# Turning probabilities and values in pieces between the weight splits of a two-layer decoder

## The chip, the cores and the metric

The kernel runs on one core of one Trainium2 chip, as one program that is launched once. The metric is the device time of that launch in microseconds (us). Five engines work side by side, each through its own list of instructions in the order in which they stand: TensorE (PE in the profile; PEld are its loads of stationary operands), VectorE (DVE), ScalarE (ACT), GpSimd (POOL) and SyncE (SP), which issues most of the transfers from memory. An engine that waits for a semaphore holds up everything that stands behind in its list.

## The reference

A decoder trunk of two layers over 272 tokens (16 learned ones and 256 of the sequence), width 2048, 16 heads of 128, feed-forward width 8192, all float32. The first layer mixes tokens by softmax attention with a decay that is learned per token, the second by stick-breaking attention; both compute blocks of queries against all keys up to the block's end. Cut to what matters here:

```python
for layer in range(DEPTH):                       # 2
    a = rms_norm(h, norm_attn[layer])
    if layer < N_A_LAYERS:                       # layer 0
        q, k, v, f_logit = split(a @ fox_w_in)
        cum_logf = cumsum(log_sigmoid(f_logit + fox_b_f))
        o = forgetting_attention(q, k, v, cum_logf)    # softmax(q k * scale + decay) @ v
        h = h + o @ fox_w_o
    else:                                        # layer 1
        c = rms_norm(h, kv_norm)
        k, v = split(c @ w_kv)
        q = a @ sb_w_q
        o = stick_breaking_attention(q, k, v)    # exp(log_sigmoid(z) + suffix sums) @ v
        h = h + o @ sb_w_o
    h = h + square(relu(rms_norm(h, norm_mlp[layer]) @ w_up[layer])) @ w_down[layer]
return rms_norm(h, final_norm)[:, N_META:]
```

## The kernel before

Activations lie feature-major: 16 chunks of 128 features by 272 tokens. All products with weights go through `gemm_group`, which makes 4 output chunks (512 columns of weights, `acc`) from all 16 input chunks, in four quarters `kb` of four input chunks each. A float32 product is made of three products of rounded parts: each weight tile `raw` is split by ACT into a rounded part `whi` (L214) and by DVE into the rest `wlo` (L215), the activations likewise into `hi` and `lo`, and PE adds hi*hi, lo*hi and hi*lo (L162). So a quarter is 4 x 4 x 3 = 48 matmuls. A quarter's weights come as two halves of 512 KB, by SP, into 4 `raw` buffers; there are 4 `whi` and 4 `wlo` buffers, so that ACT and DVE split at most two quarters ahead of PE. Quarters 0 and 3 finish one output chunk after the other, so they need both halves early; quarters 1 and 2 use one half and then the other.

Heads go in four groups `g` of four. In layer 0 a group has three gemm groups, for queries, keys and values; in layer 1 two, for keys and values, since all queries are made ahead. After the keys come the scores of the group's heads and, beside the values' gemm, the softmax or the stick-breaking sums on DVE and ACT. Both the probabilities and the values then stand the wrong way round for the product that makes the heads' outputs and are turned:

- `turned`: DVE turns each 32 x 32 square within its partitions (`sb`, L346, two instructions), then ACT moves the 16 squares of a 128 x 128 block to their places with 16 copies (`pt`, L350), each 32 partitions x 384.
- `token_major`: when the values' gemm is read out of PSUM (`vT`, L357), DVE turns them with 16 transposes of 32 x 256 (`vt`, L365).

`outputs` then multiplies `vt` by `pt` on PE (`po`, L384 to L388) and splits the result into the next operand (`x_o`, L408 and L409). It is not run at once: `small` (the corners, that is the 16 learned tokens and the last keys) and `outputs` are kept in `late`. In layer 0 `small` is queued ahead of quarter 2 of the next group of queries, and `outputs` behind that group; in layer 1, and in both out-projections, they go ahead of quarters 1 and 3 of the next gemm group.

What sets the order: each engine's list is made by a scheduler that runs when the program is built. It takes ready instructions by the order of the code and by a modelled time; `issue_after` adds that an instruction must stand behind a given one on the same engine. `gemm_group` takes functions `before` and `after` by quarter; those in `after` are traced once a quarter's splits are, under `issue_after` of that quarter's last `whi` and last `wlo`:

```python
if kb in after:
    with tc.issue_after(on_act.ins), tc.issue_after(on_dve.ins):
        after[kb]()
```

Before the change all 32 instructions of a turning are traced at one place, the copies ahead of the values' gemm and the transposes behind it.

## Time and profile before

| | us |
|---|---|
| median of 3 runs | 2320.24 |
| lowest and highest run | 2319.99, 2321.96 |
| the profiled execution | 2322.33 |
| its span, first to last instruction | 2320.6 |
| PE busy | 2280.8 |
| DVE busy | 1359.6 |
| ACT busy | 1110.3 |

The profile is of one execution. The time that the kernel is judged by is some 1.7 us longer than the span, since it holds what lies ahead of the first and behind the last instruction. A row of the timeline gives start, length, engine, line and what is written from what, and in brackets the idle time of the engine just before and what ended it. Of PE's matmuls a row's length overlaps the next one's; the pace is read from start to start. A few matmul records are missing from a trace. The granted clock of PE is given as a share of its full clock.

### The profile page before, as it was taken

What the parts mean: (1) busy time and instruction counts of PE and PEld (TensorE: products, weight loads), DVE (VectorE), ACT (ScalarE), POOL (GpSimd) and SP (SyncE); (2) the same over time, 40 slices, a digit from 0 to 9 for tenths busy, and PEclk for the clock granted to TensorE, in tenths of its full rate; (3) what the DMA queues carried; (4) which work ended last, traced back from release to release, by engine and by line L of the source; (5) the groups of instructions that cost most, each with busy time, mean ns of one, the idle gap of its engine ahead of it and who ended that gap; (6) DMA issues with size and microseconds to landing.
All of it is one profiled execution on the core that took longest, in us unless ns stands there. A gap on an engine that the chain in (4) does not pass through costs nothing.

```text
span 2320.6 us, 44744 instructions
## 1 busy us (share of the span) xinstructions
PE 2280.8 (98%) x18882; PEld 2272.9 (98%) x18882; DVE 1359.6 (59%) x1909; ACT 1110.3 (48%) x1533; POOL 27.5 (1%) x75
## 2 busy tenths in 40 slices
PE   9899999999999999999999999999999999999998
PEld 9899999999999999999999999999999999999998
DVE  7766666654455445455566677776555555555554
ACT  6553554444344345334444566655543544544553
POOL 1000000000000000000000000000000000000000
PEclk9999999999999999999999999999999999999999
DMA  7445444555555555555555544456566566565563
GB/s 239 147 147 174 155 145 160 184 168 187 176 176 182 171 186 175 183 171 184 173 182 189 177 153 146 147 172 198 184 200 193 189 200 192 191 200 191 191 200 128
DMA packets 116905, 412.32 MB, mean 178 GB/s; under 512 B 13520, under 2 KB 16992, under 8 KB 116704
## 3 DMA queue, kind: packets, MB, share of 16 engines
q1 hardware_dynamic: 114560, 406.29, 54.2%
q8 instruction: 148, 2.42, 0.4%
q10 hardware_dynamic: 2144, 3.17, 0.4%
q14 instruction: 53, 0.43, 0.1%
HBM read 407.29 MB, written 2.11 MB: 176 GB/s over the span
## 4 chain that ended last, share of the span: by engine, by line
PE 92%; DVE 2%; ACT 1%; issue 1%; DVEq 0%; ACTq 0%
PE acc L162 90%; DVE vt L365 1%; ACT pt L350 1%; DVE wlo L215 1%; PE po L384 1%; PE ps L338 0%; PE po L387 0%; PE ps L336 0%; DVE sb L346 0%; ACT whi L214 0%; PE po L388 0%; DVE ob L668 0%; DVE vT L357 0%; PE pms_fin L625 0%; DVE ob L665 0%
## 5 line engine op out<-in xcount | busy, mean ns | idle before, releaser
L215 DVE TENSOR_TENSOR wlo<-raw,whi 128x1024 fp32r<-128x1024 f32 (+1 forms) x773 | 926.6, 1216 | 714.3 <-ACT whi L214 707.4
L214 ACT ACTIVATE whi<-raw 128x1024 fp32r<-128x1024 f32 (+1 forms) x773 | 795.9, 1050 | 986.0 <-PE acc L162 935.2
L162 PE MATMUL acc<-x_m,whi 128*128 128x272 f32 (+1 forms) x4096 | 643.3, 282 | 0.0
L162 PE MATMUL acc<-x_u,whi 128*128 128x272 f32 (+1 forms) x4096 | 642.9, 282 | 0.0
L162 PEld LDWEIGHTS acc<-x_m,whi 128*128 128x128 f32 x4096 | 566.1, 188 | 0.1
L162 PEld LDWEIGHTS acc<-x_u,whi 128*128 128x128 f32 x4096 | 565.9, 188 | 0.0
L162 PE MATMUL acc<-x_m,wlo 128*128 128x272 f32 (+1 forms) x2048 | 441.1, 282 | 0.0
L162 PE MATMUL acc<-x_u,wlo 128*128 128x272 f32 (+1 forms) x2048 | 441.0, 282 | 0.0
L162 PE MATMUL acc<-x_a,whi 128*128 128x272 f32 (+1 forms) x2048 | 362.1, 290 | 8.8 <-ACT whi L214 8.8
L162 PEld LDWEIGHTS acc<-x_m,wlo 128*128 128x128 f32 x2048 | 323.5, 188 | 0.0
L162 PEld LDWEIGHTS acc<-x_u,wlo 128*128 128x128 f32 x2048 | 323.4, 188 | 0.0
L162 PEld LDWEIGHTS acc<-x_a,whi 128*128 128x128 f32 x2048 | 307.9, 193 | 10.1 <-ACT whi L214 9.9
L162 PE MATMUL acc<-x_a,wlo 128*128 128x272 f32 (+1 forms) x1024 | 258.0, 290 | 9.4 <-DVE wlo L215 9.4
L162 PE MATMUL acc<-x_kv,whi 128*128 128x272 f32 x1024 | 195.5, 290 | 0.0
L162 PEld LDWEIGHTS acc<-x_a,wlo 128*128 128x128 f32 x1024 | 179.8, 192 | 11.2 <-DVE wlo L215 10.8
L162 PE MATMUL acc<-x_o,whi 128*128 128x272 f32 (+1 forms) x1024 | 162.6, 283 | 0.7 <-ACT x_o L408 0.4
L162 PEld LDWEIGHTS acc<-x_kv,whi 128*128 128x128 f32 x1024 | 162.6, 191 | 0.0
L162 PE MATMUL acc<-x_kv,wlo 128*128 128x272 f32 x512 | 149.0, 291 | 8.1 <-DVE wlo L215 8.1
L162 PEld LDWEIGHTS acc<-x_o,whi 128*128 128x128 f32 x1024 | 141.9, 188 | 1.4 <-DVE x_o L409 0.7
L244 DVE TENSOR_TENSOR hT<-acc,hT 128x272 f32<-128x272 f32 (+1 forms) x160 | 69.0, 431 | 85.6 <-PE acc L162 85.4
L162 PE MATMUL acc<-x_o,wlo 128*128 128x272 f32 (+1 forms) x512 | 110.8, 282 | 2.1 <-DVE wlo L215 2.1
L162 PEld LDWEIGHTS acc<-x_kv,wlo 128*128 128x128 f32 x512 | 98.0, 191 | 8.7 <-DVE wlo L215 8.7
(180 smaller groups left out, 1057.9 us busy)
## 6 DMA issues: line engine op xcount, KB each, us to landing
raw<-w_up SPq DMA_DIRECT2D x256, 512.0 KB, 4.6
raw<-w_dn SPq DMA_DIRECT2D x256, 512.0 KB, 4.6
raw<-w_qkv SPq DMA_DIRECT2D x92, 512.0 KB, 4.1
raw<-w_o SPq DMA_DIRECT2D x64, 512.0 KB, 4.6
raw<-w_kv SPq DMA_DIRECT2D x64, 512.0 KB, 4.5
raw<-w_q SPq DMA_DIRECT2D x32, 512.0 KB, 4.8
fk<-f_dram ACTq DMA_DIRECT2D x4, 544.0 KB, 4.4
raw<-w_qkv SPq DMA_DIRECT2D x7, 256.0 KB, 4.5
```

The costliest lines, as they stand in the source:

```text
L162: ins = nc.tensor.matmul(*args, **kw).ins
L214: on_act = nc.scalar.activation(hp, src, AF.Copy)
L215: on_dve = nc.vector.tensor_tensor(out=lp, in0=src, in1=hp.bitcast(F32), op=ALU.subtract)
L244: nc.vector.tensor_tensor(out=hT[:, c, t0:], in0=acc, in1=hT[:, c, t0:], op=ALU.add)
L350: nc.scalar.activation(out[32 * b:32 * b + 32, :, 32 * a:32 * a + 32], sb[32 * a:32 * a + 32, :, 32 * b:32 * b + 32], AF.Copy)
L365: nc.vector.transpose(out=out[32 * b:32 * b + 32, :, :, 32 * a:32 * a + 32], in_=src[32 * a:32 * a + 32, :, :, 32 * b:32 * b + 32])
L384: ins = nc.tensor.matmul(po[:, i, :], v[:, j, 0, :], p[:, j, :2 * P], start=i == 0, stop=False)
```

## The change

`turned` and `token_major` no longer issue their instructions; each returns the output tile and a function `piece(first, last)` that issues the copies or transposes first to last. A table `PLANS` says which piece goes behind the splits of which quarter. In layer 0 copies 0 to 3 and 4 to 7 go behind quarters 2 and 3 of the group's own values gemm, the other eight behind quarters 0 and 1 of the following gemm group; in layer 1 copies 0 to 3 behind quarter 3 and the rest behind quarters 0 to 2 of the following group. The transposes go behind quarters 0, 1 and 2 of the following group: 4, 6 and 6 in layer 0, and 2, 7 and 7 in layer 1. The two DVE instructions that make `sb` go with the first copies. What follows the last group of heads is the out-projection's first gemm group. `small` and `outputs` keep their places.

```diff
+        def piece(first, last):
+            if first == 0:
+                for o, u, n in ((0, 0, P), (144, P, 2 * P)):
+                    nc.vector.transpose(out=sb.rearrange("p (h k) -> p h k", h=4)[:, :, u:u + n], in_=s[:, :, o:o + n])
+            for i in range(first, last):
+                a, b = 32 * (i // 4), 32 * (i % 4)
+                nc.scalar.activation(out[b:b + 32, :, a:a + 32], src[a:a + 32, :, b:b + 32], AF.Copy)
+
+        return pt.rearrange("p (h k) -> p h k", h=4), piece
...
-        for a in range(4):
-            for b in range(4):
-                nc.vector.transpose(out=out[32 * b:32 * b + 32, :, :, 32 * a:32 * a + 32],
-                                    in_=src[32 * a:32 * a + 32, :, :, 32 * b:32 * b + 32])
-        return vt.rearrange("p h (b t) -> p h b t", t=P)
+
+        def piece(first, last):
+            for i in range(first, last):
+                a, b = 32 * (i // 4), 32 * (i % 4)
+                nc.vector.transpose(out=out[b:b + 32, :, :, a:a + 32], in_=src[a:a + 32, :, :, b:b + 32])
+
+        return vt.rearrange("p h (b t) -> p h b t", t=P), piece
+
+    def early(turn_p, plan):
+
+        return {kb: (lambda a=a, b=b: turn_p(a, b)) for kb, (a, b) in plan.items()}
+
+    def turns(turn_p, turn_v, p, v):
+
+        def piece(kb):
+            if kb in p:
+                turn_p(*p[kb])
+            if kb in v:
+                turn_v(*v[kb])
+
+        return {kb: (lambda kb=kb: piece(kb)) for kb in range(3)}
+
+    PLANS = {0: ({2: (0, 4), 3: (4, 8)}, {0: (8, 12), 1: (12, 16)}, {0: (0, 4), 1: (4, 10), 2: (10, 16)}),
+             1: ({3: (0, 4)}, {0: (4, 8), 1: (8, 12), 2: (12, 16)}, {0: (0, 2), 1: (2, 9), 2: (9, 16)})}
...
-            gemm_group(w_qkv0[3 * g], xa, 0, evac_q, {2: late[0]})
+            gemm_group(w_qkv0[3 * g], xa, 0, evac_q, {2: late[0]}, turning)
...
-        gemm_group(w_qkv0[3 * g + 2], xa, 0, evac_v)
+        gemm_group(w_qkv0[3 * g + 2], xa, 0, evac_v, after=early(turn_p, PLANS[0][0]))
...
+        turning = turns(turn_p, turn_v, *PLANS[0][1:])
...
-            gemm_group(w[g], ao, t0, evac, {1: late[0], 3: late[1]} if g == 0 else {}, widen=t0 == M)
+            gemm_group(w[g], ao, t0, evac, {1: late[0], 3: late[1]} if g == 0 else {},
+                       turning if g == 0 else {}, widen=t0 == M)
```

The calls in layer 1 change in the same way, with `PLANS[1]`.

The built lists show where the pieces come to stand. In their names the numbers of a split are gemm group, quarter and half, and a buffer's number; `pt_0_1` is layer 0, g=1. First ACT in layer 0 at g=1, from the last quarter of the values' gemm (group 6) into the next group of queries (7). Before:

```order
L214 ACTIVATE whi_6_3_0_2037<-raw_6_3_0_2033 128x1024
L350 ACTIVATE pt_0_1_1829<-sb_0_1_1828 32x12x32 x16
L214 ACTIVATE whi_6_3_1_2041<-raw_6_3_1_2034 128x1024
L214 ACTIVATE whi_7_0_0_2129<-raw_7_0_0_2125 128x1024
L214 ACTIVATE whi_7_0_1_2133<-raw_7_0_1_2126 128x1024
L214 ACTIVATE whi_7_1_0_2189<-raw_7_1_0_2185 128x1024
L214 ACTIVATE whi_7_1_1_2193<-raw_7_1_1_2186 128x1024
```

And now:

```order
L214 ACTIVATE whi_6_3_0_2025<-raw_6_3_0_2021 128x1024
L353 ACTIVATE pt_0_1_1829<-sb_0_1_1828 32x12x32 x4
L214 ACTIVATE whi_6_3_1_2029<-raw_6_3_1_2022 128x1024
L353 ACTIVATE pt_0_1_1829<-sb_0_1_1828 32x12x32 x4
L214 ACTIVATE whi_7_0_0_2105<-raw_7_0_0_2101 128x1024
L214 ACTIVATE whi_7_0_1_2109<-raw_7_0_1_2102 128x1024
L353 ACTIVATE pt_0_1_1829<-sb_0_1_1828 32x12x32 x4
L214 ACTIVATE whi_7_1_0_2173<-raw_7_1_0_2169 128x1024
L214 ACTIVATE whi_7_1_1_2177<-raw_7_1_1_2170 128x1024
L353 ACTIVATE pt_0_1_1829<-sb_0_1_1828 32x12x32 x4
```

The sixteen copies stood ahead of the split of the second half of quarter 3; now four stand ahead of it, and the others behind three later splits or pairs of splits.

DVE at the same place, from the read-out of the values (`vT`) to the splits of the next group's quarter 3. Before:

```order
L357 TENSOR_TENSOR vT0_1_1848<-acc_6_3_1852,rstd_a0_542 128x272
L215 TENSOR_TENSOR wlo_7_1_0_2190<-raw_7_1_0_2185,whi_7_1_0_2189 128x2x512
L365 STREAM_TRANSPOSE vt_0_1_2102<-vT0_1_1848 32x4x2x32 x16
L215 TENSOR_TENSOR wlo_7_1_1_2194<-raw_7_1_1_2186,whi_7_1_1_2193 128x2x512
L215 TENSOR_TENSOR wlo_7_2_0_2264<-raw_7_2_0_2259,whi_7_2_0_2263 128x2x512
L215 TENSOR_TENSOR wlo_7_2_1_2268<-raw_7_2_1_2260,whi_7_2_1_2267 128x2x512
L215 TENSOR_TENSOR wlo_7_3_0_2324<-raw_7_3_0_2319,whi_7_3_0_2323 128x2x512
```

And now:

```order
L360 TENSOR_TENSOR vT0_1_1830<-acc_6_3_1834,rstd_a0_542 128x272
L215 TENSOR_TENSOR wlo_7_1_0_2174<-raw_7_1_0_2169,whi_7_1_0_2173 128x2x512
L370 STREAM_TRANSPOSE vt_0_1_2094<-vT0_1_1830 32x4x2x32 x4
L215 TENSOR_TENSOR wlo_7_1_1_2178<-raw_7_1_1_2170,whi_7_1_1_2177 128x2x512
L370 STREAM_TRANSPOSE vt_0_1_2094<-vT0_1_1830 32x4x2x32 x6
L215 TENSOR_TENSOR wlo_7_2_0_2258<-raw_7_2_0_2253,whi_7_2_0_2257 128x2x512
L215 TENSOR_TENSOR wlo_7_2_1_2262<-raw_7_2_1_2254,whi_7_2_1_2261 128x2x512
L370 STREAM_TRANSPOSE vt_0_1_2094<-vT0_1_1830 32x4x2x32 x6
L215 TENSOR_TENSOR wlo_7_3_0_2324<-raw_7_3_0_2319,whi_7_3_0_2323 128x2x512
```

The sixteen transposes stood between the two halves of quarter 1; now four stand there, six behind the pair and six behind quarter 2.

DVE in layer 1 at g=1, from the read-out of the values into the next group of keys (57). Before:

```order
L357 TENSOR_TENSOR vT1_1_15403<-acc_56_3_15407,rstd_a1_13533 128x272
L365 STREAM_TRANSPOSE vt_1_1_15655<-vT1_1_15403 32x4x2x32 x16
L215 TENSOR_TENSOR wlo_57_1_0_15752<-raw_57_1_0_15747,whi_57_1_0_15751 128x2x512
L215 TENSOR_TENSOR wlo_57_1_1_15756<-raw_57_1_1_15748,whi_57_1_1_15755 128x2x512
L374 TENSOR_TENSOR pm_sb_1_1_15742<-pm_1_1_15740,maskD_127 128x128
L215 TENSOR_TENSOR wlo_57_2_0_15812<-raw_57_2_0_15807,whi_57_2_0_15811 128x2x512
L215 TENSOR_TENSOR wlo_57_2_1_15816<-raw_57_2_1_15808,whi_57_2_1_15815 128x2x512
```

And now:

```order
L360 TENSOR_TENSOR vT1_1_15385<-acc_56_3_15389,rstd_a1_13533 128x272
L370 STREAM_TRANSPOSE vt_1_1_15643<-vT1_1_15385 32x4x2x32 x2
L215 TENSOR_TENSOR wlo_57_1_0_15730<-raw_57_1_0_15725,whi_57_1_0_15729 128x2x512
L215 TENSOR_TENSOR wlo_57_1_1_15734<-raw_57_1_1_15726,whi_57_1_1_15733 128x2x512
L370 STREAM_TRANSPOSE vt_1_1_15643<-vT1_1_15385 32x4x2x32 x7
L396 TENSOR_TENSOR pm_sb_1_1_15720<-pm_1_1_15718,maskD_127 128x128
L215 TENSOR_TENSOR wlo_57_2_0_15801<-raw_57_2_0_15796,whi_57_2_0_15800 128x2x512
L215 TENSOR_TENSOR wlo_57_2_1_15805<-raw_57_2_1_15797,whi_57_2_1_15804 128x2x512
L370 STREAM_TRANSPOSE vt_1_1_15643<-vT1_1_15385 32x4x2x32 x7
L215 TENSOR_TENSOR wlo_57_3_0_15888<-raw_57_3_0_15883,whi_57_3_0_15887 128x2x512
```

All splits of the next group stood behind the sixteen transposes; now two transposes stand ahead of quarter 1 and seven each ahead of quarters 2 and 3.

On ACT two of the pieces come to stand together in all four places of layer 1 and at g=0 of layer 0, where the first piece's `sb` is made late. Here layer 1 at g=1, now:

```order
L621 ACTIVATE r1_1_15335<-r1_1_15335 128x832
L214 ACTIVATE whi_57_0_1_15660<-raw_57_0_1_15653 128x1024
L353 ACTIVATE pt_1_1_15384<-sb_1_1_15383 32x12x32 x8
L214 ACTIVATE whi_57_1_0_15729<-raw_57_1_0_15725 128x1024
L214 ACTIVATE whi_57_1_1_15733<-raw_57_1_1_15726 128x1024
L353 ACTIVATE pt_1_1_15384<-sb_1_1_15383 32x12x32 x4
L214 ACTIVATE whi_57_2_0_15800<-raw_57_2_0_15796 128x1024
L214 ACTIVATE whi_57_2_1_15804<-raw_57_2_1_15797 128x1024
L353 ACTIVATE pt_1_1_15384<-sb_1_1_15383 32x12x32 x4
```

Before, the sixteen stood where the eight stand. The lists of SP and GpSimd are in the same order as before, and PE's differ by three small instructions of the corners that move by a few rows.

More of the change, by code (lines that the diff above doesn't have):

```diff
@@ L344, in turned @@
                   for t in ("sb", "pt"))
-        for o, u, n in ((0, 0, P), (144, P, 2 * P)):
-            nc.vector.transpose(out=sb.rearrange("p (h k) -> p h k", h=4)[:, :, u:u + n], in_=s[:, :, o:o + n])
-        sb, out = (t.rearrange("p (u k) -> p u k", k=P) for t in (sb, pt))
-        for a in range(4):
-            for b in range(4):
-                nc.scalar.activation(out[32 * b:32 * b + 32, :, 32 * a:32 * a + 32],
-                                     sb[32 * a:32 * a + 32, :, 32 * b:32 * b + 32], AF.Copy)
-        return pt.rearrange("p (h k) -> p h k", h=4)
+        src, out = (t.rearrange("p (u k) -> p u k", k=P) for t in (sb, pt))
+        def piece(first, last):
[6 more added lines that the diff above has]
+        return pt.rearrange("p (h k) -> p h k", h=4), piece
     def values(label):
@@ L362, in token_major @@
         out, src = (t.rearrange("p h (b t) -> p h b t", t=P) for t in (vt, vT[:, :, :2 * P]))
-        for a in range(4):
-            for b in range(4):
-                nc.vector.transpose(out=out[32 * b:32 * b + 32, :, :, 32 * a:32 * a + 32],
-                                    in_=src[32 * a:32 * a + 32, :, :, 32 * b:32 * b + 32])
-        return vt.rearrange("p h (b t) -> p h b t", t=P)
+        def piece(first, last):
[14 more added lines that the diff above has]
+             1: ({3: (0, 4)}, {0: (4, 8), 1: (8, 12), 2: (12, 16)}, {0: (0, 2), 1: (2, 9), 2: (9, 16)})}
     def corner_probs(packed, label):
@@ L411, in yoco_kernel @@
     ao = Split("o0", 0)
-    late = []
+    late, turning = [], {}
     for g in range(4):
@@ L476, in yoco_kernel @@
         sm = corners(s[:, :, P:144], s[:, :, 400:416], f"sm_0_{g}")
-        probs = turned(s, f"0_{g}")
+        probs, turn_p = turned(s, f"0_{g}")
         vT, evac_v = values(f"0_{g}")
-        gemm_group(w_qkv0[3 * g + 2], xa, 0, evac_v)
+        gemm_group(w_qkv0[3 * g + 2], xa, 0, evac_v, after=early(turn_p, PLANS[0][0]))
         vm, vc = packed(vT[:, :, 0:32], f"vm_{g}"), corners(vT[:, :, P:144], vT[:, :, 256:T], f"vc_{g}")
-        vals = token_major(vT, f"0_{g}")
+        vals, turn_v = token_major(vT, f"0_{g}")
         vm_sb = tmp.tile([P, T], F32, tag="relu", name=f"vm_sb_{g}")[:, :2 * P]
@@ L497, in small, with out_proj @@
             put_split(ao, 4 * g, 4, 0, M, po[:, :P].rearrange("p (h q) -> p h q", h=4)[:, :, :M])
+        turning = turns(turn_p, turn_v, *PLANS[0][1:])
         late = [small, lambda g=g, probs=probs, vals=vals, vm_sb=vm_sb, box=box:
                 outputs(g, ao, probs, vals, box["pm"], vm_sb[:, P:], f"0_{g}")]
-    def out_proj(w, ao, t0, gi, label, late):
+    def out_proj(w, ao, t0, gi, label, late, turning):
         norm = Norm(label, t0)
@@ L541, in mlp @@
                 gemm_group(w_dn[layer, f, g], u, t0, evac, widen=t0 == M and g % 2 == 1)
-    xm, norm_m = out_proj(w_o0, ao, 0, G_M0, "m0", late)
+    xm, norm_m = out_proj(w_o0, ao, 0, G_M0, "m0", late, turning)
     norm1 = Norm("a1", 0)
@@ L574, in yoco_kernel @@
     ao = Split("o1", M)
-    late = []
+    late, turning = [], {}
     for g in range(4):
         kT, ks, evac_k = keys(f"1_{g}")
-        gemm_group(w_kv[2 * g], xc, 0, evac_k, {1: late[0], 3: late[1]} if late else {})
+        gemm_group(w_kv[2 * g], xc, 0, evac_k, {1: late[0], 3: late[1]} if late else {}, turning)
         q = qT1[g]
@@ L598, in yoco_kernel @@
         sm = corners(r[:, :, P:144], r[:, :, 400:416], f"sm_1_{g}")
-        probs = turned(r, f"1_{g}")
+        probs, turn_p = turned(r, f"1_{g}")
         vT, evac_v = values(f"1_{g}")
-        gemm_group(w_kv[2 * g + 1], xc, 0, evac_v)
+        gemm_group(w_kv[2 * g + 1], xc, 0, evac_v, after=early(turn_p, PLANS[1][0]))
         vc = corners(vT[:, :, P:144], vT[:, :, 256:T], f"vc1_{g}")
-        vals = token_major(vT, f"1_{g}")
+        vals, turn_v = token_major(vT, f"1_{g}")
         vm_sb = tmp.tile([P, T], F32, tag="relu", name=f"vm1_sb_{g}")[:, :P]
@@ L612, in small @@
             nc.scalar.copy(vm_sb, pv[:, :P])
+        turning = turns(turn_p, turn_v, *PLANS[1][1:])
         late = [small, lambda g=g, probs=probs, vals=vals, vm_sb=vm_sb, box=box:
                 outputs(g, ao, probs, vals, box["pm"], vm_sb, f"1_{g}")]
-    xm, norm_m = out_proj(w_o1, ao, M, G_M1, "m1", late)
+    xm, norm_m = out_proj(w_o1, ao, M, G_M1, "m1", late, turning)
     pms = patt.tile([P, 512], F32, tag="patt", name="pms_fin")
```

## The prediction

> **What bounds the kernel now.** I read the page first, then the stages, then what TensorE (PE) waited for, then the timelines of ACT and DVE ahead of those waits. The page gives the busy time of each engine and, for its costliest groups, busy time, mean ns of one instruction, and idle time before them:

> ```profile
> PE 2280.8 (98%) x18882; PEld 2272.9 (98%) x18882; DVE 1359.6 (59%) x1909; ACT 1110.3 (48%) x1533; POOL 27.5 (1%) x75
> L215 DVE TENSOR_TENSOR wlo<-raw,whi 128x1024 fp32r<-128x1024 f32 (+1 forms) x773 | 926.6, 1216 | 714.3 <-ACT whi L214 707.4
> L214 ACT ACTIVATE whi<-raw 128x1024 fp32r<-128x1024 f32 (+1 forms) x773 | 795.9, 1050 | 986.0 <-PE acc L162 935.2
> ```

> PE is the bound, and ACT mostly waits for PE to free split buffers. But 98% is an average. Stages (window, length, then busy time of PE, PEld, DVE, ACT and POOL, the granted clock of PE, DMA share, GB/s):

> ```profile
> 93.00:376.00 283.00, 270.21 (x2078) 267.02 (x2079) 178.02 (x332) 132.85 (x220) 10.85 (x18) 0.96 0.48 157
> 460.00:1217.00 757.00, 757.00 (x6147) 756.96 (x6146) 396.81 (x484) 327.49 (x419) 0.32 (x2) 1.00 0.55 178
> 1317.00:1540.00 223.00, 213.00 (x1681) 210.91 (x1680) 167.30 (x251) 142.91 (x197) 3.58 (x18) 0.98 0.46 151
> ```

> The first MLP keeps PE busy all 757 us at full clock. The attention stage of each layer (first and third row) does not, and loses clock too. The waits of PE in 93 to 376 us (two rows) and in 1317 to 1540 us (total, times, longest):

> ```profile
> PE acc L162 <- DVE wlo L215: 9.9, 7, 5.7
> PE acc L162 <- ACT whi L214: 6.5, 3, 2.2
> PE acc L162 <- DVE wlo L215: 9.6, 4, 2.7
> ```

> All are for split weights. They sit at the eight places where a group of heads is turned (16 ACT copies for probabilities, 16 DVE transposes for values, all at once). The first place straddles 93 us; there ACT, DVE and PE show:

> ```profile
> 78.85 8.53 ACT L350 ACTIVATE pt<-sb 32x384 f32<-32x384 f32 x16 [1.01 <-DVE sb L346]
> 86.21 7.18 DVE L365 STREAM_TRANSPOSE vt<-vT 32x256 f32<-32x256 f32 x16
> 88.51 0.51 PE L162 MATMUL acc<-x_a,whi 128*128 128x272 f32 x2 [2.08 <-ACT whi L214]
> 94.70 0.60 PE L162 MATMUL acc<-x_a,wlo 128*128 128x272 f32 x1 [5.67 <-DVE wlo L215]
> ```

> PE first waits 2.08 us for a split behind the copies, then 5.67 us for one behind the transposes. The second place (layer 0, g=1; ACT, then DVE, then PE) is the pattern of g=1 to 3:

> ```profile
> 158.35 1.06 ACT L214 ACTIVATE whi<-raw 128x1024 fp32r<-128x1024 f32 x1 [0.40 <-PE acc L162]
> 160.56 8.53 ACT L350 ACTIVATE pt<-sb 32x384 f32<-32x384 f32 x16 [1.15 <-DVE st L472]
> 169.12 2.95 ACT L214 ACTIVATE whi<-raw 128x1024 fp32r<-128x1024 f32 x3
> ...
> 159.29 1.23 DVE L346 STREAM_TRANSPOSE sb<-s 128x1024 f32<-128x1024 f32 x1
> 170.21 3.50 DVE L215 TENSOR_TENSOR wlo<-raw,whi 128x1024 fp32r<-128x1024 f32 x3 [8.31 <-ACT whi L214]
> 180.72 7.18 DVE L365 STREAM_TRANSPOSE vt<-vT 32x256 f32<-32x256 f32 x16
> 187.92 3.50 DVE L215 TENSOR_TENSOR wlo<-raw,whi 128x1024 fp32r<-128x1024 f32 x3
> ...
> 167.53 0.41 PE L162 MATMUL acc<-x_a,whi 128*128 128x272 f32 x2
> 167.77 0.29 PE L162 MATMUL acc<-x_a,wlo 128*128 128x272 f32 x1
> 170.23 0.82 PE L162 MATMUL acc<-x_a,whi 128*128 128x272 f32 x2 [2.17 <-ACT whi L214]
> 171.49 0.60 PE L162 MATMUL acc<-x_a,wlo 128*128 128x272 f32 x1 [0.44 <-DVE wlo L215]
> 171.88 0.66 PE L162 MATMUL acc<-x_a,whi 128*128 128x272 f32 x2
> 172.33 0.43 PE L162 MATMUL acc<-x_a,wlo 128*128 128x272 f32 x1
> 189.21 0.39 PE L162 MATMUL acc<-x_a,wlo 128*128 128x272 f32 x1 [0.89 <-DVE wlo L215]
> ```

> The copies hold back the last split of the values' group (2.17 us), the transposes one of the next group (0.89 us). Before the wait two matmuls take 0.24 us, start to start (167.53 to 167.77), so 0.123 each; after it 0.45 us (171.88 to 172.33), so 0.225: each wait also leaves a slow stretch. The slow stretches, with PE's busy time and granted clock (six; the first, the last and the sum):

> ```profile
> 94.70:98.49 3.79, 3.79 (x17) 0.50 0.70 202
> 1466.78:1470.66 3.88, 3.88 (x19) 0.56 0.68 209
> sum 26.24, PE 26.24; mean PE 4.37
> ```

> In layer 1 the wait comes from the transposes alone (g=1; ACT, DVE, PE):

> ```profile
> 1395.89 8.54 ACT L350 ACTIVATE pt<-sb 32x384 f32<-32x384 f32 x16 [0.80 <-DVE sb L346]
> ...
> 1400.62 7.18 DVE L365 STREAM_TRANSPOSE vt<-vT 32x256 f32<-32x256 f32 x16
> 1407.83 2.36 DVE L215 TENSOR_TENSOR wlo<-raw,whi 128x1024 fp32r<-128x1024 f32 x2
> 1410.11 0.28 DVE L374 TENSOR_TENSOR pm_sb<-pm,maskD 128x128 f32<-128x128 f32 x1
> ...
> 1409.11 0.55 PE L162 MATMUL acc<-x_kv,wlo 128*128 128x272 f32 x1 [2.69 <-DVE wlo L215]
> ```

> **The change, part by part.** No arithmetic is added or removed; 128 copies and 128 transposes change their places. A copy costs 8.53/16 = 0.53 us of ACT, a transpose 7.18/16 = 0.45 us of DVE, a split 1.05 us of ACT and about 1.2 of DVE. A quarter of a group is 48 matmuls, 48 x 0.123 = 5.9 us of PE. Pieces are pinned behind a quarter's splits, so I ask at each place whether the splits behind the pieces still come before PE wants them.

> Layer 0, g=1. PE wanted the held split at 170.23 - 2.17 = 168.06, six matmuls into quarter 3, which thus began at 167.3. In the new order four copies (2.1 us) run from 160.6 to 162.7, the split's ACT half to 163.8, its DVE half to 165.0: 3 us early, so the 2.17 and 0.44 go. Quarter 3 then ends at 173.2. Behind it DVE does the split of the next quarter 1 (ready 175.5, wanted 179.1), four transposes (177.3), its second half (178.5, wanted 182), six transposes (181.2), the two of quarter 2 (183.6; the first, at 182.4, is wanted at 185.0), six transposes (186.3), those of quarter 3 (188.8, wanted 190.9). Spare times of 2 us and more: the 0.89 goes. ACT's last two pieces fall into gaps in which it waited for PE. g=2 and 3 repeat this.

> Layer 0, g=0. Eight copies still stand ahead of a split: 78.85 + 4.3 = 83.1, split to 84.2 on ACT and 85.4 on DVE; wanted at 88.51 - 2.08 = 86.4. Spare: 1.0 us, the least of all. The splits of quarter 1 follow after four transposes at 90.4, wanted from 91.6. So 2.08 and 5.67 go.

> Layer 1, g=1. The values' last chunk is read out at 1400.5 here as before. Two transposes (1401.4), the splits of quarter 1 (1403.8; wanted at 1409.11 - 2.69 = 1406.4), seven transposes (1407.0), the corner product (0.28), splits of quarter 2 (1409.5, wanted from 1411.8), seven transposes (1412.7), splits of quarter 3 (1415.2, wanted 1417.9). ACT does eight copies together here too, but ends them at 1400.2, in time. The 2.69 goes; the other three places alike.

> Cover: the pieces hide under PE's quarters. In layer 1 DVE's fullest quarter holds two splits 2.4, seven transposes 3.1 and the corner product 0.28, so 5.8 of 5.9 us; without that 0.1 us each excess would show at PE. The weights' loads on SP keep their order. A raw buffer is released by its split, so pieces ahead of a split delay the load two quarters on: in layer 0 the split that ends at 178.5 frees a buffer whose content is wanted at 185 by ACT,

> ```profile
> raw<-w_qkv SPq DMA_DIRECT2D x92, 512.0 KB, 4.1
> ```

> and 4.1 us after issue it is there at 182.6. GpSimd's and SP's rows keep their order, and PE's only shift two small transposes and a product of the corners by a few rows; I cost these at nothing, since full quarters of gemm stand around them. What is late next: in each layer's out-projection PE still waits for the attention output's own split, 0.3 and 0.4 us:

> ```profile
> PE acc L162 <- DVE x_o L409: 0.3, 1, 0.3
> PE acc L162 <- ACT x_o L408: 0.4, 1, 0.4
> ```

> Those are another chain and stay.

> Unknown: the price of breaking a string of 16 into pieces. From below nothing: one engine does the same instructions in turn. From above, each piece pays a hand-over like the 0.1 us gaps, and where the spare is below that, PE waits as much: three pieces at eight places, 2.4 us. I take nothing, since spares are 1 to 3 us, and keep 2.4 for the range.

> Sum. Waits: 9.9 + 6.5 + 2.1 (the 2.08 before 93 us) + 9.6 = 28.1 us. Slow stretches: at 0.123 instead of 0.225 the 26.24 us take 14.3, so 11.9 us less. Together 40.0. The few matmuls next to a wait are slow as well (171.49 to 171.88 is 0.39 for one): some 14 of these at 0.2 would add 3, which I keep for the range. The profiled execution took 2322.33 us, its span 2320.6; it lies 2.1 above the median of 2320.24, and the gain is taken from the median: 2280.

> [...]

> **Rivals.**
> (a) Part of the waits stays. The order is written by the program, but the spare at g=0 is 1.0 us and DVE's fullest quarter has 0.1. If each place keeps 1 us of wait, 8 come back: 2288; if half the slow stretches stay with them, 6 more: 2294. Against it: no spare comes out negative.
> (b) The slow stretches are not the waits' doing and stay, but for the first (3.79 x 0.453 = 1.7): 2320.2 - 28.1 - 1.7 = 2290. Against it: they all start right after a wait, and 757 us without a wait have none. [...]
> (c) Slower: DVE can't hold its pieces. If a transpose ahead of a split takes longer where it is alone between splits, each of three quarters at eight places overruns. It decides from 40/24 = 1.7 us per quarter on, when DVE's 5.8 would be 7.5. At 2 us per quarter, 48 us of waits: 2328. For it: DVE is all but full there; against it: 425 to 443 ns in all 128 transposes:

> ```profile
> L365 DVE STREAM_TRANSPOSE vt<-vT x128: 425/436/443, 86.2 to 1522.7; 32x256 f32<-32x256 f32 x128
> ```

> (d) The change does nothing, since PE is the bound and waits move to the next splits: 2320. Against it: the waits stand in PE's own row, and PE never idles where no turning stands.

> **Numbers.** Forecast 0.74 (2274 to 2286); (a) 0.11; (b) 0.05; (c) 0.06; (d) 0.04. Time 2280. The range goes from the forecast's low end (3 us of restarts, 2 of spread, so 2274) up to (a) with its clock, 2294, and leaves out (c) and (d). Faster by over 0.2% (4.6 us, about what a measurement tells from no change) 0.90, within 0.04, slower 0.06.

> **What would show it.** In the changed profile PE's waits for wlo and whi between 86 and 376 and between 1317 and 1540 us are gone and the x_o ones stay; granted clock 1.00 in both stages; copies in fours and eights and transposes in fours, sixes, twos and sevens between splits; DVE and ACT busy as before to 1%. The forecast is wrong if PE shows new waits for wlo right behind a piece, for a raw load, or at po behind vt.

## The result: 42 us faster, and TensorE all but full

| | us |
|---|---|
| before, median (4 runs beside the changed kernel) | 2320.76 (2319.99 to 2321.96) |
| after, median (4 runs) | 2278.87 (2278.47 to 2278.99) |
| ratio after/before | 0.9819, 95% interval 0.9802 to 0.9836 |
| profiled execution of after, its span | 2278.99, 2277.3 |

The forecast was 2280 (2274 to 2294). The profile after gives the same three groups on its page, with busy time, mean ns and idle time before them:

```profile
PE 2265.0 (99%) x18882; PEld 2259.6 (99%) x18882; DVE 1360.6 (60%) x1909; ACT 1111.8 (49%) x1533; POOL 32.8 (1%) x75
...
L215 DVE TENSOR_TENSOR wlo<-raw,whi 128x1024 fp32r<-128x1024 f32 (+1 forms) x773 | 927.4, 1216 | 674.1 <-ACT whi L214 666.9
L214 ACT ACTIVATE whi<-raw 128x1024 fp32r<-128x1024 f32 (+1 forms) x773 | 797.3, 1051 | 942.5 <-PE acc L162 909.5
L162 PE MATMUL acc<-x_m,whi 128*128 128x272 f32 (+1 forms) x4096 | 643.2, 281 | 0.0
```

DVE and ACT do as much as before (1360.6 against 1359.6, and 1111.8 against 1110.3); they only do it elsewhere. PE's busy time is 15.8 us less (2280.8 to 2265.0) for the same 18882 products: 11.9 of it is work done at half clock (0.50 to 0.56 in the six slow stretches of before) that is no longer there, and the rest is the matmuls next to a wait (worked out below). The two attention stages, whose limits have moved with the kernel (window, length, then PE, PEld, DVE, ACT, POOL, granted clock, DMA share, GB/s):

```profile
86.00:360.00 274.00, 273.67 (x2199) 272.53 (x2199) 193.33 (x359) 145.93 (x238) 16.74 (x21) 1.00 0.53 170
1280.00:1500.00 220.00, 219.60 (x1768) 218.38 (x1768) 173.71 (x263) 148.28 (x205) 3.61 (x18) 1.00 0.49 161
```

PE is busy for all but 0.3 and 0.4 us of them, at clock 1.00 (before 0.96 and 0.98). PE's waits over the whole span (total, times, longest) say what is left:

```profile
PE pr_fin L682 <- DVE fin L676: 1.3, 1, 1.3
PE idle L62 <- DVE mean_w L58: 1.1, 1, 1.1
PE acc L162 <- ACT x_o L430: 0.4, 1, 0.4
PE acc L162 <- ACT whi L214: 0.4, 1, 0.4
PE acc L162 <- DVE x_o L431: 0.3, 1, 0.3
PE pms_fin L650 <- ACT sq_fin L662: 0.3, 1, 0.3
```

The first, the second and the last are the kernel's end, start and end; the one for `whi` is at 18.61 us, before any turning. In the attention stages only the two waits for `x_o` are left, as foretold. Layer 0, g=1, DVE, from the last read-out of the values on, with the pieces between the splits:

```profile
164.29 0.44 DVE L360 TENSOR_TENSOR vT<-acc,rstd_a 128x272 f32<-128x272 f32 x1 [1.04 <-PE acc L162]
164.64 1.22 DVE L215 TENSOR_TENSOR wlo<-raw,whi 128x1024 fp32r<-128x1024 f32 x1
165.78 1.78 DVE L370 STREAM_TRANSPOSE vt<-vT 32x256 f32<-32x256 f32 x4
167.58 1.23 DVE L215 TENSOR_TENSOR wlo<-raw,whi 128x1024 fp32r<-128x1024 f32 x1
168.84 2.68 DVE L370 STREAM_TRANSPOSE vt<-vT 32x256 f32<-32x256 f32 x6
171.56 2.36 DVE L215 TENSOR_TENSOR wlo<-raw,whi 128x1024 fp32r<-128x1024 f32 x2
173.95 2.70 DVE L370 STREAM_TRANSPOSE vt<-vT 32x256 f32<-32x256 f32 x6
```

The order is the one worked out, and a transpose costs no more in a piece: 2.70/6 = 0.45 us, as 7.18/16 before.

Where the time came out is seen at the first product of the statistics, at the start of the first layer's attention (`pms_a`) and at the MLP norm of both layers (`pms_m`; first and last of its products). Before, then after:

```profile
L143 PE MATMUL pms_a<-ssq_a,mean_w x4: 390/392/393, 36.8 to 1217.0; 128*128 128x272 f32 x4
L143 PE MATMUL pms_m<-ssq_m,mean_w x4: 378/385/392, 459.5 to 1619.9; 128*128 128x272 f32 x2, 128*128 128x256 f32 x2
```

```profile
L143 PE MATMUL pms_a<-ssq_a,mean_w x4: 390/392/392, 37.8 to 1187.7; 128*128 128x272 f32 x4
L143 PE MATMUL pms_m<-ssq_m,mean_w x4: 378/384/391, 430.2 to 1577.0; 128*128 128x272 f32 x2, 128*128 128x256 f32 x2
```

The start is 1.0 us later. Layer 0's attention takes 422.7 - 392.4 = 30.3 us less, layer 1's 1619.9 - 459.5 - (1577.0 - 430.2) = 13.6 less, together 43.9; less the 1.0, that is the 43.3 by which the span fell, within 0.5. By the medians it is 41.9, since the profiled execution of before lies 1.6 us above its median and that of after 0.1.

### The profile page after: what moved, and what is told of

Its sections match the earlier page's. It is cut to its first block, busy times and chain, and to the rows that moved or that the text cites. A ratio compares the mean times of both kernels' runs of the same rounds, so it can differ in the third digit from the quotient of the medians.

```text
span 2277.3 us, 44746 instructions
## 1 busy us (share of the span) xinstructions
PE 2265.0 (99%) x18882; PEld 2259.6 (99%) x18882; DVE 1360.6 (60%) x1909; ACT 1111.8 (49%) x1533; POOL 32.8 (1%) x75
## 4 chain that ended last, share of the span: by engine, by line
PE 99%; DMA 1%; DVE 0%; ACT 0%; issue 0%; DVEq 0%; SPq 0%; ACTq 0%
PE acc L162 96%; PE po L406 1%; PE ps L338 1%; DMA raw<-w_qkv 1%; PE ps L336 0%; PE po L409 0%; DMA hT<-hT_in 0%; PE po L410 0%; DVE ob L693 0%; PE pf L285 0%; PE pf L286 0%; ACT whi L214 0%; PE pms_fin L650 0%; DVE ob L690 0%; ACT x_o L430 0%; PE pms_a L143 0%
## 5 line engine op out<-in xcount | busy, mean ns | idle before, releaser
L215 DVE TENSOR_TENSOR wlo<-raw,whi 128x1024 fp32r<-128x1024 f32 (+1 forms) x773 | 927.4, 1216 | 674.1 <-ACT whi L214 666.9
L214 ACT ACTIVATE whi<-raw 128x1024 fp32r<-128x1024 f32 (+1 forms) x773 | 797.3, 1051 | 942.5 <-PE acc L162 909.5
L162 PE MATMUL acc<-x_m,whi 128*128 128x272 f32 (+1 forms) x4096 | 643.2, 281 | 0.0
L162 PE MATMUL acc<-x_u,whi 128*128 128x272 f32 (+1 forms) x4096 | 642.9, 281 | 0.0
L162 PEld LDWEIGHTS acc<-x_m,whi 128*128 128x128 f32 x4096 | 566.0, 188 | 0.1
L162 PEld LDWEIGHTS acc<-x_u,whi 128*128 128x128 f32 x4096 | 565.8, 188 | 0.0
L162 PE MATMUL acc<-x_m,wlo 128*128 128x272 f32 (+1 forms) x2048 | 440.9, 281 | 0.0
L162 PE MATMUL acc<-x_u,wlo 128*128 128x272 f32 (+1 forms) x2048 | 440.8, 281 | 0.0
L162 PE MATMUL acc<-x_a,whi 128*128 128x272 f32 (+1 forms) x2048 | 353.6, 286 | 0.5 <-ACT whi L214 0.4
L162 PEld LDWEIGHTS acc<-x_m,wlo 128*128 128x128 f32 x2048 | 323.4, 188 | 0.0
L162 PEld LDWEIGHTS acc<-x_u,wlo 128*128 128x128 f32 x2048 | 323.3, 188 | 0.0
L162 PEld LDWEIGHTS acc<-x_a,whi 128*128 128x128 f32 x2048 | 300.5, 188 | 1.5 <-ACT whi L214 1.3
L162 PE MATMUL acc<-x_a,wlo 128*128 128x272 f32 (+1 forms) x1024 | 253.1, 285 | 0.0
L162 PE MATMUL acc<-x_kv,whi 128*128 128x272 f32 x1024 | 192.6, 287 | 0.0
L162 PEld LDWEIGHTS acc<-x_a,wlo 128*128 128x128 f32 x1024 | 175.6, 188 | 0.7 <-issue 0.5
L162 PE MATMUL acc<-x_o,whi 128*128 128x272 f32 (+1 forms) x1024 | 162.6, 283 | 0.7 <-ACT x_o L430 0.4
L162 PEld LDWEIGHTS acc<-x_kv,whi 128*128 128x128 f32 x1024 | 160.0, 188 | 0.0
L162 PE MATMUL acc<-x_kv,wlo 128*128 128x272 f32 x512 | 147.1, 287 | 0.0
L162 PEld LDWEIGHTS acc<-x_o,whi 128*128 128x128 f32 x1024 | 142.0, 188 | 1.4 <-DVE x_o L431 0.7
L244 DVE TENSOR_TENSOR hT<-acc,hT 128x272 f32<-128x272 f32 (+1 forms) x160 | 69.1, 432 | 86.3 <-PE acc L162 86.2
L162 PE MATMUL acc<-x_o,wlo 128*128 128x272 f32 (+1 forms) x512 | 110.5, 282 | 0.0
L162 PEld LDWEIGHTS acc<-x_kv,wlo 128*128 128x128 f32 x512 | 96.5, 188 | 0.0
## 6 DMA issues: line engine op xcount, KB each, us to landing
raw<-w_up SPq DMA_DIRECT2D x256, 512.0 KB, 4.6
raw<-w_dn SPq DMA_DIRECT2D x256, 512.0 KB, 4.6
raw<-w_qkv SPq DMA_DIRECT2D x92, 512.0 KB, 3.8
raw<-w_o SPq DMA_DIRECT2D x64, 512.0 KB, 4.3
raw<-w_kv SPq DMA_DIRECT2D x64, 512.0 KB, 4.5
raw<-w_q SPq DMA_DIRECT2D x32, 512.0 KB, 4.7
```

What stands on the lines that cost most here:

```text
L162: ins = nc.tensor.matmul(*args, **kw).ins
L214: on_act = nc.scalar.activation(hp, src, AF.Copy)
L215: on_dve = nc.vector.tensor_tensor(out=lp, in0=src, in1=hp.bitcast(F32), op=ALU.subtract)
L244: nc.vector.tensor_tensor(out=hT[:, c, t0:], in0=acc, in1=hT[:, c, t0:], op=ALU.add)
```

## The experiments

The theory: each wait was a split standing in an in-order queue behind a string of 16, and each slow stretch was set off by such a wait; cut short enough to fit the spare time ahead of each split, the turning costs PE nothing. The rivals: one of the two strings does all the harm, the later place and not the cutting is what helps, the slow stretches have another cause, or the pieces still cost something. Each kernel is the changed one with the edit shown.

**One string at a time.** The values in pieces, the copies at once:

```diff
+        piece(0, 16)
         return pt.rearrange("p (h k) -> p h k", h=4), piece
...
+    PLANS = {0: ({}, {}, {0: (0, 4), 1: (4, 10), 2: (10, 16)}),
+             1: ({}, {}, {0: (0, 2), 1: (2, 9), 2: (9, 16)})}
```

> Only the values are turned in pieces; the sixteen copies of the probabilities stand together as before. Theory (PE waits for splits that stand behind a turning, and its clock halves after the longer of these waits): the waits behind the copies come back: 3.1 us at g=0 of layer 0 (a split ends at 90.7, wanted at 87.6), about 2.7 at g=1 to 3, 0.7 at each place of layer 1 (split of quarter 1 ready at 1374.5, wanted at 1373.7), together 14 us, and the slow stretches of layer 0 with them, 8.5 us: 2279 + 22 = 2301. Rival (only the transposes on DVE matter, since DVE is the fuller engine): 2279 to 2283. Rival (slow stretches have another cause than waits): 2293, with no slow stretch.

And the probabilities in pieces, the transposes at once:

```diff
+        piece(0, 16)
         return vt.rearrange("p h (b t) -> p h b t", t=P), piece
...
+    PLANS = {0: ({2: (0, 4), 3: (4, 8)}, {0: (8, 12), 1: (12, 16)}, {}),
+             1: ({3: (0, 4)}, {0: (4, 8), 1: (8, 12), 2: (12, 16)}, {})}
```

> Only the probabilities are turned in pieces; the sixteen transposes of the values stand together as before. Theory: the waits behind the transposes stay: 3.0 us at g=0 of layer 0, 1.8 at g=1 to 3 (second half of quarter 1 ready at 183.9, wanted at 182.1 on the clock of the kernel before), 2.7 at three places of layer 1 and 1.5 at the last, 18 us, with slow stretches of some 5 us in layer 1 and at g=0: 2279 + 23 = 2302. Rival (the copies alone were the cause): 2279 to 2283. Rival (cutting one of the two strings wins everything, because the other is then hidden): below 2285.

Measured: 2301.62 us (2300.62 to 2303.96), ratio to before 0.9923 (0.9908 to 0.9938), and 2302.55 us (2301.82 to 2303.22), 0.9925 (0.9911 to 0.9940). PE's waits for splits, with the copies whole:

```profile
PE acc L162 <- ACT whi L214: 8.8, 5, 2.2
PE acc L162 <- DVE wlo L215: 4.2, 7, 0.7
```

and with the transposes whole:

```profile
PE acc L162 <- DVE wlo L215: 13.5, 8, 2.8
```

So each string alone keeps its own waits: the copies 12.8 us (of the 13.0 recorded, 0.24 stand at 7.4 us, before any turning), four times 2.1 to 2.2 and then 0.74 in layer 0 and 0.39 at three places in layer 1; the transposes 13.5, 2.7 us at each of three places in layer 1, 0.3 at the fourth and 0.5 to 2.8 in layer 0. Both parts of the change are needed. That both forecast times were met is partly luck: waits and slow stretches were put at 14 + 8.5 and 18 + 5 us and came to 12.8 + 5.6 and 13.5 + 7.5, and the matmuls next to a wait and longer waits for `x_o`, which the forecasts had left out, made up the rest.

The two gains, 18.4 and 17.5 us, add to 35.9 and not to the 41.2 of the whole change by the same median of before (2320.02). A part of the difference lies in the slow stretches: PE was busy at half clock for 12.4 and 16.6 us, together 29.0, where before had 26.2. Either string alone leaves a slow stretch at g=0 of layer 0 (clock 0.66 over 89 to 94 us with the copies whole, 0.53 over 95.5 to 99 with the transposes whole), and the transposes alone leave one at all four places of layer 1 (0.58, 0.66, 0.66 and 0.52 in windows of 3.5 to 5 us), where before had two. At 0.225 instead of 0.123 us per matmul that is 1.3 us; the other 4 aren't assigned.

**The later place without the cutting.** All 16 copies and all 16 transposes, uncut, behind the splits of quarter 1 of the following group:

```diff
+    PLANS = {0: ({}, {1: (0, 16)}, {1: (0, 16)}),
+             1: ({}, {1: (0, 16)}, {1: (0, 16)})}
```

> Both turnings stay whole strings of sixteen, but stand behind the splits of quarter 1 of the following group. Theory (it is the length of a string between two quarters' splits that counts, not the place): DVE makes sb only here, ACT's copies start 1.9 us later and end after 8.5, and the first split of quarter 2 is ready some 4.2 us after PE wants it, at each of eight places: 34 us of waits and up to 14 us of slow stretches, 2313 to 2327. Rival (moving the string behind the next splits is what helps, pieces are not needed): 2279 to 2285.

Measured: 2320.22 us (2317.52 to 2323.04), ratio 1.0001 (0.9991 to 1.0010). The waits came back behind the copies:

```profile
PE acc L162 <- ACT whi L214: 17.9, 8, 3.4
PE acc L162 <- DVE wlo L215: 5.1, 7, 0.7
```

At layer 0, g=1, the string on ACT and what PE waited for behind it:

```profile
172.81 8.53 ACT L353 ACTIVATE pt<-sb 32x384 f32<-32x384 f32 x16 [3.44 <-DVE sb L350]
181.37 3.90 ACT L214 ACTIVATE whi<-raw 128x1024 fp32r<-128x1024 f32 x4
...
182.48 0.52 PE L162 MATMUL acc<-x_a,whi 128*128 128x272 f32 x2 [1.61 <-ACT whi L214]
```

Moving the strings to this place is worth nothing; cutting them is. The waits are 23.0 us against 28.1 before (and against the 34 forecast), the span of the profiled execution 2318.1 against 2320.6: a part of what the shorter waits gave went into slow stretches, with PE busy at half clock for 29.7 us against 26.2; the granted clock is 0.991 over the span in both.

**Where the pieces start.** All copies behind the following group's quarters, in eights or fives and sixes, none in the values' own group:

```diff
+    PLANS = {0: ({}, {0: (0, 8), 1: (8, 16)}, {0: (0, 4), 1: (4, 10), 2: (10, 16)}),
+             1: ({}, {0: (0, 6), 1: (6, 11), 2: (11, 16)}, {0: (0, 2), 1: (2, 9), 2: (9, 16)})}
```

> Pieces as in the changed kernel, but no copies inside the values' own group: eight and eight behind quarters 0 and 1 of the following group in layer 0, six, five and five in layer 1. Theory (spares of 1 to 3 us; eight copies are 4.3 us of ACT against 5.9 of PE's quarter less 2.1 of splits, so 0.5 us over, taken from the spare): no wait, 2278 to 2281. Rival (the gain hangs on the start inside the values' group): over 2285, with waits for whi at quarter 1.

Measured: 2279.09 us (2278.36 to 2279.28), ratio 0.9823 (0.9807 to 0.9840): the same as the change. The waits in the attention stages are the two for `x_o`. This other table does as well; it holds no piece that is longer than the spare time, and eight copies fit it:

```profile
162.11 4.27 ACT L353 ACTIVATE pt<-sb 32x384 f32<-32x384 f32 x8 [3.04 <-DVE sb L350]
166.41 2.02 ACT L214 ACTIVATE whi<-raw 128x1024 fp32r<-128x1024 f32 x2
168.45 4.26 ACT L353 ACTIVATE pt<-sb 32x384 f32<-32x384 f32 x8
```

**How much spare there is, and what the clock does.** Behind quarter 1 of each following group, 8, 12 or 16 of the transposes are done a second time, into the same places, so that the piece there grows from 6 or 7 to as many as 23. The case with 8:

```diff
                 turn_v(*v[kb])
+            if kb == 1:
+                turn_v(0, 8)
```

> Eight of the transposes are done a second time in the piece behind quarter 1 at each of the eight places (same result): 8 x 0.449 = 3.6 us more of DVE there. Theory: the first split of quarter 2 had 2.6 us to spare in layer 0 (3.3 at g=0) and 3.5 in layer 1, so PE waits 1.0 us at three places, 0.3 at g=0 and 0.1 in layer 1, no slow stretch: 2279 + 4 = 2283. Rival (DVE has no spare, as its fullest quarter holds 5.8 of 5.9 us): 8 x 3.6 = 29 us, 2308.

With `turn_v(0, 12)`:

> Twelve transposes done a second time behind quarter 1. By the lists 16 to 18 transposes stand ahead of the first split of quarter 2 instead of six or seven. Theory: waits of 1.3 us at g=0, 2.3 to 2.7 at the other places of layer 0 and 1.4 in layer 1, 14 us in all. If the clock falls after waits of 2.2 us and up, as in the kernel before, three slow stretches add 6 us: 2299. [...] Rival (no spare): 8 x 5.4 = 43 us and more, over 2322.

With `turn_v(0, 16)`:

> All sixteen transposes done a second time behind quarter 1: 7.2 us more of DVE at each place. Theory: waits of 4.6 us at three places of layer 0, 3.9 at g=0 and 3.7 in layer 1, 32 us, and a slow stretch of about 2 us lost behind each: 2279 + 32 + 16 = 2327; 2311 if slow stretches are not the waits' doing. Rival (no spare): 8 x 7.2 = 58 us, 2336 without slow stretches.

| repeated at each place | median us (lowest, highest) | ratio to before (95%) | over the change |
|---|---|---|---|
| 8 | 2283.74 (2282.88 to 2284.24) | 0.9840 (0.9823 to 0.9856) | 4.9 |
| 12 | 2294.94 (2294.65 to 2295.82) | 0.9888 (0.9873 to 0.9902) | 16.1 |
| 16 | 2326.15 (2325.11 to 2327.41) | 1.0025 (1.0016 to 1.0034) | 47.3 |

The same 32 transposes of DVE work (4 more at 8 places, 14 us) cost PE 11 us in the one step and 31 in the next. With 16, layer 0, g=1, DVE and PE:

```profile
174.31 10.07 DVE L370 STREAM_TRANSPOSE vt<-vT 32x256 f32<-32x256 f32 x22
184.41 2.36 DVE L215 TENSOR_TENSOR wlo<-raw,whi 128x1024 fp32r<-128x1024 f32 x2
...
185.69 0.60 PE L162 MATMUL acc<-x_a,wlo 128*128 128x272 f32 x1 [3.61 <-DVE wlo L215]
186.09 0.66 PE L162 MATMUL acc<-x_a,whi 128*128 128x272 f32 x2
186.54 0.43 PE L162 MATMUL acc<-x_a,wlo 128*128 128x272 f32 x1
```

16 x 0.449 = 7.2 us more work made a wait of 3.6, so 3.6 us had been spare. Behind the wait two matmuls take 0.45 us (186.09 to 186.54), the slow pace of before. With 12, layer 1, g=0, and the clock behind the wait (window, length, PE busy, clock, DMA share, GB/s):

```profile
1326.60 8.34 DVE L370 STREAM_TRANSPOSE vt<-vT 32x256 f32<-32x256 f32 x18
...
1336.45 0.39 PE L162 MATMUL acc<-x_kv,wlo 128*128 128x272 f32 x1 [1.44 <-DVE wlo L215]
1336.68 0.41 PE L162 MATMUL acc<-x_kv,whi 128*128 128x272 f32 x2
1336.92 0.29 PE L162 MATMUL acc<-x_kv,wlo 128*128 128x272 f32 x1
...
1336.00:1343.00 7.00, 6.55 (x51) 1.00 0.49 150
```

Here the pace behind the wait is full (1336.68 to 1336.92 for two) and the clock 1.00, at this and at the seven other places. PE's waits for `wlo` in the two runs, with 12 and then with 16:

```profile
PE acc L162 <- DVE wlo L215: 11.2, 9, 1.4
```

```profile
PE acc L162 <- DVE wlo L215: 28.2, 8, 3.8
```

So from 12 to 16 each place waits about 2 us longer, as DVE's 1.8 us make it, and slow stretches cost the rest, (31.2 - 17.0)/8 = 1.8 us a place. The granted clock over the span is 0.998 with 12, as after the change, and 0.990 with 16. That shows the cause of the slow stretches: the same string, four transposes longer, brings them back. The waits set them off, behind transposes here (3.61 us, then 0.50 over 185.69 to 188.80) and behind copies in the runs above, and the short ones, 1.0 to 1.45 us with 12, don't. With 12, the forecast of 2299 was missed by 4 us: the waits came out at 1.0 to 1.45 us, since the spare ahead of the first split of quarter 2 is 3.4 to 4.4 us by the two runs, more than I had worked out, and the three slow stretches of the forecast didn't come.

With 8 the recorded waits are small, 0.01 to 0.15 us ahead of the splits and two longer ones ahead of the second out-projection:

```profile
PE acc L162 <- DVE x_o L433: 1.0, 2, 0.7
PE po L408 <- DVE vt L370: 0.5, 1, 0.5
```

In the attention stages and behind them they are 1.7 us more than in the change, against 3.9 us of span. Most of the other 2.2 is what a recorded wait leaves out. At seven of the eight places PE shows a short wait ahead of the first split of quarter 2; there the start of the held matmul lies 0.30 to 0.43 us behind the start before it, and the next start 0.23 or 0.24 us behind it, where the pace is 0.123. At g=0 of layer 0, for one, the held matmul starts at 99.09 and the next at 99.32. Summed over the seven places that is 2.4 us beyond the pace, with 0.5 recorded as idle. So the time of 2283 was met, but not by the waits of 1.0 us that were forecast.

**No turning at all.** The copies and transposes are left out; the probabilities and the values go into the heads' outputs as zeros that GpSimd writes.

```diff
         def piece(first, last):
             if first == 0:
+                nc.gpsimd.memset(pt, 0.0)
...
         def piece(first, last):
+            if first == 0:
+                nc.gpsimd.memset(vt, 0.0)
```

> The turning is left out: no transposes and no copies, the turned tiles are set to zero by GpSimd instead, so the outputs of attention are not the reference's. Theory (in the changed kernel the turning costs PE nothing any more): 2278 to 2280, as with it. Rival (pieces still cost PE something that no wait shows, by pace or by hand-over): below 2276.

Measured: 2279.20 us (2278.82 to 2279.80), ratio 0.9820 (0.9805 to 0.9834), against 2278.87 for the change. The turning in pieces is worth nothing more: 67 us of ACT and 56 of DVE lie wholly beside PE's products, so no other table of pieces is to be expected to gain anything.

## Why the prediction was right

**The waits, 28.1 us.** All gone, at all eight places, and none came up elsewhere in the two attention stages. The undone halves bring them back where the order says they should be.

**The slow stretches, 11.9 us.** Gone too, and caused by the waits, as assumed: they came back with 16 repeated transposes (clock 0.990 over the span) and stood at none of the eight places with 12 (1.00 at each). Rival (b), that they have another cause, falls: it was put at 2290, and 2278.87 was measured. That the first stretch alone would go with the waits, the 1.7 us in that sum, no run shows; all six went, 11.9 us, and five of them stood at waits of 2.6 to 2.9 us.

**The few matmuls next to a wait, up to 3 us.** This is the term that was mis-sized: it was kept for the range and belonged in the sum. It has two parts, and the prediction saw one. The matmul behind a wait is slow: with 12 repeated transposes it takes 0.23 us to the next start (1336.45 to 1336.68) where the pace is 0.123, and at half clock 0.39 (171.49 to 171.88 in the kernel before) where the pace is 0.225. Beyond what the slow stretches already count, that is about 0.1 us for each of the 15 waits, 1.5 in all. And each wait costs the overlap with the matmul before it, which the prediction didn't have: one lasts 0.281 us (the page's mean) where the pace is 0.123, and only what is idle beyond its end is recorded. 15 waits at 0.16 are 2.4 us. With both the sum is 28.1 + 11.9 + 2.4 + 1.5 = 43.9, and the two attention stages gave 43.9; the last three terms are the 15.8 us by which PE's busy time fell. By layers the sum without the matmuls next to a wait was 18.5 + 8.5 = 27.0 and 9.6 + 3.4 = 13.0 (stretches of 18.8 and 7.4 us, at 0.453), measured 30.3 and 13.6: eleven of the fifteen waits stood in layer 0, and at 0.26 each the two layers come to 29.9 and 14.0.

**The start.** It took 1.0 us more in the profiled execution and gave that back from the gain. It is no doing of the change: the same product starts at 36.9 us in the kernel with whole strings and at 37.9 in the one with 12 repeated transposes, which are alike up to there.

**A string broken into pieces, 0 to 2.4 us, taken as nothing.** Right: leaving the turning out changes the time by 0.3 us, no more than the runs spread, and a transpose takes 436 ns in the change as before.

**The spare times.** At g=0 of layer 0, with 1.0 us the least, there was no wait. Ahead of quarter 2 I had 2.6 us for layer 0 and, by 1408.4 against 1411.8 when worked the same way, 3.4 for layer 1; the repeated transposes measured 3.4 to 4.4 in layer 0 and 3.4 to 3.9 in layer 1. The hand-worked spare was short by about 1 us in layer 0, on the safe side.

**Rival (a), part of the waits stays,** did not happen, for the spare times were real. **Rival (c), DVE can't hold its pieces,** did not happen either, and its deciding point was set too low: 1.7 us per quarter was the whole gain spread over 24 quarters, as if every overrun showed at PE at once. Over three quarters that is 5.1 us a place, and 12 x 0.449 = 5.4 us a place, all in one quarter, cost 16 us and not 40. The runs show that a quarter can overrun by 8 x 0.449 = 3.6 us at each place for 4.9 us in all, and that it is as slow as before only from about 16 x 0.449 = 7.2 us on. **Rival (d), no effect,** is out by the ratio; its mechanism, waits that only move on, is what the uncut strings behind quarter 1 did.

## What to carry to other kernels

In the in-order queues of this kernel the length of a string mattered against the spare time of what stands behind it, and not the engine's busy share: DVE at 59% and ACT at 48% held up a PE that was 98% busy. Look for the feed of the bound engine behind a string that is longer than its spare, cut the string to fit between two feeds, and don't expect that moving it whole will help: here it gave nothing. When adding up what a wait costs, count the idle time, the lost overlap and the slow matmul beside it, and the matmuls at low clock after it: here 28, 4 and 12 us.

## What the hardware showed that was not expected

After waits of 2.6 us and more the granted clock fell, but not always. In the kernel before, seven places waited 2.6 us and more in all, and six of them have a slow stretch; at g=0 of layer 1, with 2.69 us, and at the last place, with 1.54, the clock stayed at 1.00. The eight places with 12 repeated transposes, which waited 1.0 to 1.45 us, kept 1.00, and with the copies whole so did g=1 of layer 0, with 2.92.

```profile
161.59:165.01 3.42, 1.80 (x15) 1.00 0.00 0
165.01:168.42 3.41, 2.11 (x15) 1.00 0.16 34
243.51:246.93 3.42, 1.25 (x9) 1.00 0.00 0
246.93:253.76 6.83, 6.08 (x27) 0.50 0.62 181
```

The other exception, g=0 of layer 1 before the change, was cut the same way, into 0.85 and 1.84 us. In the attention stages of the kernel before, all six falls came at the end of a cell in which PE was idle for 2.1 to 2.9 us, and cells with up to 1.84 us kept the clock. With the transposes whole, 1.53 us was enough in a cell with ten products, some of them the short ones of the outputs; why isn't shown:

```profile
1515.30:1518.71 3.41, 1.88 (x10) 1.00 0.52 157
1518.71:1522.12 3.41, 3.41 (x18) 0.50 0.56 189
```

The longest wait goes by the same count. At g=0 of layer 0 before the change, the clock fell at 91.64, with 3.1 us of the 5.67 still to wait and 2.9 us idle in the cell before. So this stretch began within the wait and not only behind it.
